# Conditioning rows summed over partitions by VectorE block turns and one small matmul, with the bias as a first row of the sum

## The chip, the core and the metric

The kernel runs on one core of a Trainium2 chip. The metric is the device time of one execution in microseconds (us). The engines spoken of are TensorE (PE in the profile, with PEld for its weight loads), VectorE (DVE), ScalarE (ACT), GpSimd (POOL) and SyncE (SP), whose queue issues nearly all DMA transfers. Every engine works through its own instructions strictly in order.

## The reference

Two transformer stacks of two layers each run one after the other on 256 tokens of width 1024; the first one also carries 256 context tokens through its first layer. Every layer is steered by a conditioning vector: a matrix-vector product gives six rows of 1024 values, of which two shift (`sh`), two scale (`sc`) and two gate (`g`) the layer.

```python
mod = silu_c @ w_ada[l] + b_ada[l]            # 1024 x 6144, once per layer (and once for the context)
sh_a, sc_a, g_a, sh_f, sc_f, g_f = jnp.split(mod[:, None, :], 6, axis=-1)
hx = rmsnorm(x) * (1 + sc_a) + sh_a
...                                           # mixing layer, attention and so on
x = x + g_a * (mixed @ w_out[l])
x = x + g_f * swiglu(rmsnorm(x) * (1 + sc_f) + sh_f, w_gate[l], w_up[l], w_down[l])
# swiglu(h, wg, wu, wd) = (silu(h @ wg) * (h @ wu)) @ wd,  1024 -> 2816 -> 1024
```

All is fp32.

## The kernel before

**Weights.** A large matrix product is cut into weight chunks. `weights` loads a chunk (`raw`, 128x1024 for two row blocks of 512 columns; some are 768 or 512 wide), ScalarE rounds it to `whi` (L170) and VectorE takes the rest, `wlo = raw - whi` (L171, both in `split`). TensorE multiplies each piece three times: high by high, high by low, low by high (L177, L178, L179 in `mm3`). In the first feed-forward each of `raw`, `whi` and `wlo` has three buffers, so a chunk can be made ready while TensorE works on one of the two before. In the later feed-forwards spoken of here there are six for the high and low parts. A chunk of two row blocks in the first feed-forward (four groups of 128 tokens) is 24 matmuls of 512 columns.

**Modulations beside the matmuls.** Some of the conditioning rows are worked out in small steps beside the three feed-forwards that come before their use. `ada_one` is a Python generator for one job, one row of 1024 values: for each of eight blocks `k` it loads 128x1024 of the matrix (`adaw`, three buffers) and VectorE accumulates `acc += adaw * cs` (L358, the first block with L356), `cs` holding 128 values of the conditioning vector, one for each partition. A job for two vectors (the main and the context tokens) has two `acc`, both fed from one `adaw`. Then the bias is added in partition 0 (L364) and the sum over the 128 partitions is taken:

- for a gate (`g`): two halves, each split into `acchi` and `acclo` and multiplied on TensorE by a matrix of ones (L372, L373);
- for a shift or scale (`sh`, `sc`), which is needed as a column of 128 partitions by 8: eight TensorE transposes of 128x128 in two groups of four (L382), each group followed by four ScalarE copies that sum along the row (L387, `colj`, into `cols`); then one VectorE copy (`col_out`, L249 or L251).

**Order.** `tick` is called once for each weight chunk and adds `rate` to a counter; for each whole number in it one step of the front job is emitted, up to its next `yield`. The first feed-forward (`ffn0`, about 298 to 668 us) has 12 jobs at 1.8 steps for each of its 64 chunks, three of them with two `acc`; the second (`1`, about 860 to 1060 us) has five at 0.75, the third (`b0`, about 1160 to 1300 us) two at 0.45. That makes 19 jobs with 22 `acc`: 14 for shifts and scales, 8 for gates. `ffn` empties the list of jobs before its last product (`tick(all_=True)`, L828 and L831). From the stream that comes of it a scheduler with its own estimates of time fixes the order on every engine when the kernel is built; the orders shown below are its result.

```python
def tick(self, all_=False):
    self.due += self.rate
    while self.jobs and (all_ or self.due >= 1.0):
        self.due -= 1.0
        if next(self.jobs[0], "end") == "end":
            self.jobs.pop(0)
```

Of the kernel before, what the change touches and what calls it, by code (L numbers as in the profile page):

```python
# [12 lines left out]
F32 = mybir.dt.float32  # L13
F32R = mybir.dt.float32r
U32 = mybir.dt.uint32
AF = mybir.ActivationFunctionType
ALU = mybir.AluOpType
AX = mybir.AxisListType
PSUM = bass.MemoryType.PSUM

P = 128
D = 1024
KT = D // P
# [71 lines left out]
class Net:  # L95
# [90 lines left out]
    def setup(self, fp):  # L186
        nc, A, cp = self.nc, self.A, self.cp
        self.ident = self.t(cp, [P, P], F32, "ident")
        make_identity(nc, self.ident)
        self.ones = self.t(cp, [P, P], F32R, "ones")  # L190
        nc.vector.tensor_scalar(self.ones, self.ident, 0.0, 1.0, op0=ALU.mult, op1=ALU.add)
        self.mhalf = self.t(cp, [P, 16], F32, "mhalf")
        nc.vector.memset(self.mhalf, -0.5)

        self.cs = self.t(cp, [P, 24], F32, "cs")
        self.bcol = self.t(cp, [P, 6, KT], F32, "bcol")
        with self.tc.tile_pool(name="rows", bufs=1) as rp:
            rows = self.t(rp, [64, P], F32, "rows")
            cols = lambda a: a.rearrange("(k p) -> k p", p=P)
            for i, s in ((0, A["c"][0]), (1, A["c_ctx"]), (2, A["b_ada"][0])):  # L200
                n = s.shape[0] // P
                nc.scalar.dma_start(out=rows[8 * i : 8 * i + n], in_=cols(s))
            ps = self.tr_bank()
            nc.tensor.transpose(ps[:, :64], rows, self.ident[:64, :64])
            nc.scalar.activation(self.cs[:, :16], ps[:, :16], AF.Silu)
            nc.vector.tensor_copy(self.bcol, ps[:, 16:64].rearrange("p (j k) -> p j k", j=6))

        self.cs32 = self.t(fp, [P, KT, 32], F32, "cs32")
        nc.vector.memset(self.cs32, 0.0)
        nc.vector.tensor_copy(  # L210
            self.cs32[:, :, :2], self.cs[:, :16].rearrange("p (c k) -> p k c", c=2)
        )

        self.pick = self.t(cp, [P, 2], F32, "pick")
        nc.vector.reduce_sum(
            self.pick, self.ident.rearrange("p (g m) -> p m g", g=4)[:, :2], axis=AX.X
        )
        self.sel = self.t(fp, [P, 2, P], F32, "sel")
        nc.vector.tensor_copy(self.sel, self.pick.unsqueeze(2).to_broadcast([P, 2, P]))
# [120 lines left out]
    def ada_one(self, pool, w, b, j, pairs):  # L340


        nc = self.nc
        kind = ("sh", "sc", "g")[j % 3]
        dests = [self.mod_dest(m, j, pool if c == 1 else None) for m, c in pairs]
        accs = [self.t(pool, [P, D], F32, "acc", bufs=2) for _ in pairs]
        brow = self.t(pool, [1, D], F32, "brow", bufs=1)
        nc.sync.dma_start(out=brow, in_=b[j * D : j * D + D].unsqueeze(0))
        for k in range(KT):
            raw = self.t(pool, [P, D], F32, "adaw", bufs=3)  # L350
            nc.sync.dma_start(out=raw, in_=w[k * P : k * P + P, j * D : j * D + D])
            for acc, (_, c) in zip(accs, pairs):
                s = self.cs[:, c * 8 + k : c * 8 + k + 1]
                with self.tc.issue_after(self.anchor):
                    if k == 0:
                        nc.vector.tensor_scalar_mul(acc, raw, s)  # L356
                    else:
                        nc.vector.scalar_tensor_tensor(  # L358
                            acc, raw, s, acc, op0=ALU.mult, op1=ALU.add
                        )  # L360
                if k > 0:
                    yield
        for acc, dest in zip(accs, dests):
            nc.vector.tensor_add(acc[0:1], acc[0:1], brow)  # L364
            if kind == "g":
                for h in range(2):
                    s = slice(h * 512, h * 512 + 512)
                    hi = self.t(pool, [P, 512], F32R, "acchi", bufs=1)
                    lo = self.t(pool, [P, 512], F32R, "acclo", bufs=1)
                    self.split(hi, lo, acc[:, s])  # L370
                    ps = self.ac_bank()
                    nc.tensor.matmul(ps, self.ones, hi, start=True, stop=False)  # L372
                    nc.tensor.matmul(ps, self.ones, lo, start=False, stop=True)  # L373
                    nc.scalar.copy(dest[:, s], ps)
            else:
                junk = self.t(pool, [P, P], F32, "colj", bufs=1)
                cols = self.t(pool, [P, KT], F32, "cols", bufs=2)
                for h in range(2):
                    ps = self.ac_bank()
                    for i in range(4):  # L380
                        k = 4 * h + i
                        nc.tensor.transpose(  # L382
                            ps[:, i * P : i * P + P], acc[:, k * P : k * P + P], self.ident
                        )
                    for i in range(4):
                        k = 4 * h + i
                        nc.scalar.activation(  # L387
                            junk, ps[:, i * P : i * P + P], AF.Copy, accum_out=cols[:, k : k + 1]
                        )
                self.col_out(kind, cols, dest)  # L390

    def side_jobs(self, jobs=(), rate=0.0):

# [1487 lines left out]
```

## Time and profile before

| what | value |
|---|---|
| median of 3 runs | 1702.78 us (1700.35 to 1704.63) |
| the profiled execution | 1704.78 us |
| its span, first to last instruction | 1703.0 us |
| mean granted TensorE clock | 0.990 of full speed |
| busy: PE, DVE, ACT, POOL | 96%, 72%, 50%, 3% of the span |

The span leaves out 1.8 us of the profiled execution's time. That execution lies 2.0 us above the median of the runs. Busy shares are means over stages with different limits; a stage has to be read by itself.

### The profile page before, as it was taken

The page shows a single profiled execution, that of the slowest core. Times are in us where ns is not written, and L with a number is a line of the kernel's source. Part 1 is how long each engine was busy: PE and PEld are TensorE (multiplying, and loading weights), DVE is VectorE, ACT ScalarE, POOL GpSimd, SP SyncE. Part 2 cuts the span into 40 slices and gives each one's busy share as a digit, 9 for nine tenths or more (in the row PEclk, how much of TensorE's full clock was granted, in tenths as well). Part 3 has the DMA queues.
Part 4 walks back from the last instruction along what each step waited for, and adds up shares of the span by engine and source line. Part 5 has one row for each costly group of instructions (what it writes and reads, how often), then busy time and mean ns, then how long its engine had stood idle before and what let it go on. Part 6 is the DMA issues. An engine that isn't in the chain of part 4 may idle for free.

```text
span 1703.0 us, 25231 instructions
## 1 busy us (share of the span) xinstructions
PE 1637.8 (96%) x9299; PEld 1313.0 (77%) x9299; DVE 1221.2 (72%) x2042; ACT 854.0 (50%) x1697; POOL 44.7 (3%) x53
## 2 busy tenths in 40 slices
PE   8999999999999999999999999999999999899998
PEld 5777767877777877787678878777877888778886
DVE  4558866886978877878768887887766567575555
ACT  4445664533333334555764455686544456564443
POOL 0001100000000000101000000000000000000000
PEclk9999999999999999999999999999999999999999
DMA  9550415554778786522268887434875543255653
GB/s 319 188 174 26 159 60 189 179 191 143 226 234 299 253 275 208 163 79 89 71 202 287 302 311 250 152 122 124 260 247 179 188 137 92 83 177 168 203 166 115
DMA packets 169474, 310.35 MB, mean 182 GB/s; under 512 B 12163, under 2 KB 72819, under 8 KB 169350
## 3 DMA queue, kind: packets, MB, share of 16 engines
q1 hardware_dynamic: 168966, 308.17, 56.3%
q8 instruction: 73, 1.20, 0.3%
q10 hardware_dynamic: 384, 0.56, 0.1%
q14 instruction: 51, 0.42, 0.1%
HBM read 307.64 MB, written 1.05 MB: 181 GB/s over the span
## 4 chain that ended last, share of the span: by engine, by line
PE 71%; DVE 10%; DMA 9%; ACT 5%; issue 3%; POOL 1%; SPq 0%; POOLq 0%; ACTq 0%; DVEq 0%
PE bank L179 19%; PE bank L177 19%; PE bank L178 19%; DVE wlo L171 3%; ACT whi L170 2%; PE bank L936 2%; DMA raw<-w_up 2%; PE bank L863 2%; DVE acc L358 1%; DMA adaw<-w_ada 1%; DMA raw<-w_gate 1%; PE bank L1478 1%; PE bank L321 1%; PE bank L1004 1%; ACT colj L387 1%
## 5 line engine op out<-in xcount | busy, mean ns | idle before, releaser
L170 ACT CAST whi<-raw 128x1024 fp32r<-128x1024 f32 (+2 forms) x420 | 400.5, 959 | 521.7 <-PE bank L179 239.7
L171 DVE TENSOR_TENSOR wlo<-raw,whi 128x1024 fp32r<-128x1024 f32 (+2 forms) x420 | 463.6, 1109 | 247.0 <-ACT whi L170 239.6
L177 PE MATMUL bank<-whi,hh 128*128 128x512 f32 (+2 forms) x1200 | 445.1, 374 | 10.7 <-ACT hh L170 5.8
L178 PE MATMUL bank<-wlo,hh 128*128 128x512 f32 (+2 forms) x1200 | 443.5, 370 | 2.1 <-DVE wlo L171 2.1
L179 PE MATMUL bank<-whi,hl 128*128 128x512 f32 (+2 forms) x1200 | 442.2, 371 | 0.2 <-DVE hl L171 0.2
L177 PEld LDWEIGHTS bank<-whi,hh 128*128 128x128 f32 x1200 | 228.0, 191 | 50.1 <-ACT hh L170 7.8
L179 PEld LDWEIGHTS bank<-whi,hl 128*128 128x128 f32 x1200 | 229.0, 191 | 36.1 <-DVE hl L171 3.5
L178 PEld LDWEIGHTS bank<-wlo,hh 128*128 128x128 f32 x1200 | 229.0, 191 | 33.8 <-DVE wlo L171 3.2
L358 DVE SCALAR_TENSOR_TENSOR acc<-adaw,cs,acc 128x1024 f32<-128x1024 f32 x154 | 196.0, 1279 | 18.1 <-DMA adaw<-w_ada 8.8
L178 PE MATMUL bank<-wlo,acth 128*128 128x512 f32 x440 | 174.5, 397 | 0.5 <-DVE wlo L171 0.5
L177 PE MATMUL bank<-whi,acth 128*128 128x512 f32 x440 | 174.9, 398 | 0.0
L179 PE MATMUL bank<-whi,actl 128*128 128x512 f32 x440 | 173.6, 395 | 0.0
L177 PE MATMUL bank<-hh,whi 128*128 128x512 f32 (+1 forms) x376 | 143.3, 382 | 0.0
L178 PE MATMUL bank<-hl,whi 128*128 128x512 f32 (+1 forms) x376 | 143.0, 381 | 0.0
L179 PE MATMUL bank<-hh,wlo 128*128 128x512 f32 (+1 forms) x376 | 142.5, 382 | 0.2 <-DVE wlo L171 0.2
L179 PEld LDWEIGHTS bank<-whi,actl 128*128 128x128 f32 x440 | 83.2, 189 | 18.6
L177 PEld LDWEIGHTS bank<-whi,acth 128*128 128x128 f32 x440 | 83.2, 189 | 18.5
L178 PEld LDWEIGHTS bank<-wlo,acth 128*128 128x128 f32 x440 | 83.2, 189 | 18.5 <-DVE wlo L171 0.9
L179 PEld LDWEIGHTS bank<-hh,wlo 128*128 128x128 f32 x376 | 70.1, 188 | 15.1 <-DVE wlo L171 0.4
L178 PEld LDWEIGHTS bank<-hl,whi 128*128 128x128 f32 x376 | 70.6, 188 | 14.4
L177 PEld LDWEIGHTS bank<-hh,whi 128*128 128x128 f32 x376 | 70.5, 188 | 14.5
L736 DVE TENSOR_TENSOR rtmp<-bank,gate 128x512 f32<-128x512 f32 x68 | 46.5, 686 | 32.4 <-PE bank L179 32.4
(297 smaller groups left out, 1867.6 us busy)
## 6 DMA issues: line engine op xcount, KB each, us to landing
adaw<-ada_w SPq DMA_DIRECT2D x96, 512.0 KB
adaw<-w_ada SPq DMA_DIRECT2D x80, 512.0 KB
raw<-ffn_w_in SPq DMA_DIRECT2D x64, 512.0 KB
raw<-w_down SPq DMA_DIRECT2D x46, 512.0 KB
raw<-ffn_w_out SPq DMA_DIRECT2D x40, 512.0 KB
raw<-w_gate SPq DMA_DIRECT2D x32, 512.0 KB
raw<-w_up SPq DMA_DIRECT2D x32, 512.0 KB
raw<-w_in SPq DMA_DIRECT2D x56, 256.0 KB
```

The source lines that it names most:

```text
L170: a = self.nc.scalar.copy(hi, src)
L171: b = self.nc.vector.tensor_sub(lo, src, hi.bitcast(F32))
L177: mm(out, lh, rh, start=start, stop=False)
L178: mm(out, lh, rl, start=False, stop=False)
L179: mm(out, ll, rh, start=False, stop=stop)
L321: nc.tensor.matmul(ps[h][32 * g : 32 * g + 32], self.cs32[:, k0 + g], raws[g][:, h * 512 : h * 512 + 512], start=k0 == 0, stop=k0 > 0,)
L358: nc.vector.scalar_tensor_tensor(acc, raw, s, acc, op0=ALU.mult, op1=ALU.add)
L387: nc.scalar.activation(junk, ps[:, i * P : i * P + P], AF.Copy, accum_out=cols[:, k : k + 1])
L736: nc.vector.tensor_mul(tmp[:, :nw], ps[:, :nw], gate[:, n0 : n0 + nw])
L863: self.nc.tensor.transpose(ps[:, i * P : i * P + P], ps_in[:, i * P : i * P + P], self.ident)
L936: self.nc.tensor.matmul(o[e * 64 : e * 64 + 64], v, pt[:, e::2, i], start=i == 0, stop=i == len(vs) - 1)
L1004: nc.tensor.transpose(ps[:, h * P : h * P + P], qn[:, h0 + h].bitcast(F32), self.ident)
```

## The change

The sum over partitions for a shift or scale is taken in another way. VectorE turns `acc` in blocks of 32 by 32 (`nc.vector.transpose`, STREAM_TRANSPOSE, 128x1024) and sums along each block's row (TENSOR_REDUCE to 128x32): that leaves four partial sums for each value, one in each group of 32 partitions. Then the job yields, and at its next step one matmul of 128x128 by 32 columns with the constant `fold` adds the four, and four small copies of 32 partitions by 8 spread the result out. Gates keep their matmuls with ones, with a `yield` after each split.

The bias is no longer added at the end: `brow` is now 128x1024, set to zero by GpSimd with the bias loaded into its row 0, and the first accumulation takes it as its addend (so L356 and L364 go, and every block is a SCALAR_TENSOR_TENSOR). The yields change too: one for each block `k`, for all `acc` of the job at once, where before there was one for each `acc` and block except the first. With the yields at the end, a job with one `acc` has 10 steps (shift, scale) or 11 (gate) in place of 8, and one with two has 11 or 13 in place of 15. The rates are as before.

```diff
+        self.fold = self.t(cp, [P, 4, 32], F32, "fold")
+        nc.vector.reduce_sum(
+            self.fold[:, 0], self.ident.rearrange("p (a i) -> p i a", a=4), axis=AX.X
+        )
+        nc.vector.tensor_copy(
+            self.fold[:, 1:], self.fold[:, :1].to_broadcast([P, 3, 32])
+        )
...
-        brow = self.t(pool, [1, D], F32, "brow", bufs=1)
-        nc.sync.dma_start(out=brow, in_=b[j * D : j * D + D].unsqueeze(0))
+        brow = self.t(pool, [P, D], F32, "brow", bufs=1)
+        nc.gpsimd.memset(brow, 0.0)
+        nc.sync.dma_start(out=brow[0:1], in_=b[j * D : j * D + D].unsqueeze(0))
...
                 with self.tc.issue_after(self.anchor):
-                    if k == 0:
-                        nc.vector.tensor_scalar_mul(acc, raw, s)
-                    else:
-                        nc.vector.scalar_tensor_tensor(
-                            acc, raw, s, acc, op0=ALU.mult, op1=ALU.add
-                        )
-                if k > 0:
-                    yield
+                    nc.vector.scalar_tensor_tensor(
+                        acc, raw, s, acc if k else brow, op0=ALU.mult, op1=ALU.add
+                    )
+            yield
         for acc, dest in zip(accs, dests):
-            nc.vector.tensor_add(acc[0:1], acc[0:1], brow)
             if kind == "g":
...
                     self.split(hi, lo, acc[:, s])
+                    yield
                     ps = self.ac_bank()
...
-                junk = self.t(pool, [P, P], F32, "colj", bufs=1)
-                cols = self.t(pool, [P, KT], F32, "cols", bufs=2)
-                for h in range(2):
-                    ps = self.ac_bank()
-                    for i in range(4):
-                        k = 4 * h + i
-                        nc.tensor.transpose(
-                            ps[:, i * P : i * P + P], acc[:, k * P : k * P + P], self.ident
-                        )
-                    for i in range(4):
-                        k = 4 * h + i
-                        nc.scalar.activation(
-                            junk, ps[:, i * P : i * P + P], AF.Copy, accum_out=cols[:, k : k + 1]
-                        )
-                self.col_out(kind, cols, dest)
+                turned = self.t(pool, [P, D], F32, "colj", bufs=1)
+                part = self.t(pool, [P, 32], F32, "cols", bufs=2)
+                nc.vector.transpose(turned, acc)
+                nc.vector.reduce_sum(
+                    part, turned.rearrange("p (b j) -> p b j", j=32), axis=AX.X
+                )
+                yield
+                ps = self.ac_bank()
+                nc.tensor.matmul(
+                    ps[:, :32], self.fold.rearrange("p a i -> p (a i)"), part, start=True, stop=True
+                )
+                for a in range(4):
+                    r = slice(32 * a, 32 * a + 32)
+                    self.col_out(
+                        kind, ps[r, :32].rearrange("p (k a) -> p a k", a=4)[:, a], dest[r]
+                    )
```

Line numbers of the changed kernel are 8 to 10 higher than those of before: L358 becomes L365, L443 L452, L457 L466, L474 L483, L736 and L737 become L745 and L746; the turn is L386, its reduction L387, the fold matmul L392. Numbers at the end of a name count the program's buffers and differ a little between the two.

**Place A, VectorE at the start of the first feed-forward.** Before, between the low parts of its second and third weight chunk (`wlo_3563`, `wlo_3597`; `xn` and `ynorm` are the normalised rows of the residual, `hl` their low parts, `rstd` a reciprocal root):

```order
L171 TENSOR_TENSOR wlo_3563<-raw_3560,whi_3562 128x1024
L443 TENSOR_SCALAR rstd_3431<-ss_3428 128x1
L358 SCALAR_TENSOR_TENSOR acc_3526<-adaw_3533,cs_82,acc_3526 128x1024
L457 TENSOR_SCALAR xn_3427<-resx_3027,rstd_3431 128x512 x2
L358 SCALAR_TENSOR_TENSOR acc_3525<-adaw_3567,cs_82,acc_3525 128x1024
L474 TENSOR_SCALAR ynorm_3441<-bank_688_3436,cols_0x_106 128x256
L474 TENSOR_SCALAR ynorm_3451<-bank_690_3446,cols_0x_106 128x256
L171 TENSOR_TENSOR wlo_3597<-raw_3594,whi_3596 128x1024
```

Now, ending with the same chunk's low part under its new name `wlo_3602`:

```order
L452 TENSOR_SCALAR rstd_3434<-ss_3431 128x1
L365 SCALAR_TENSOR_TENSOR acc_3529<-adaw_3567,cs_85,acc_3529 128x1024
L466 TENSOR_SCALAR xn_3430<-resx_3030,rstd_3434 128x512 x2
L365 SCALAR_TENSOR_TENSOR acc_3528<-adaw_3571,cs_85,acc_3528 128x1024
L483 TENSOR_SCALAR ynorm_3444<-bank_689_3439,cols_0x_109 128x256
L483 TENSOR_SCALAR ynorm_3454<-bank_691_3449,cols_0x_109 128x256
L365 SCALAR_TENSOR_TENSOR acc_3529<-adaw_3571,cs_85,acc_3529 128x1024
L171 TENSOR_TENSOR hl_2405<-ynorm_3444,hh_2404 128x2x256
L171 TENSOR_TENSOR hl_2405<-ynorm_3454,hh_2404 128x2x256
L483 TENSOR_SCALAR ynorm_3464<-bank_693_3459,cols_0x_109 128x256
L483 TENSOR_SCALAR ynorm_3474<-bank_695_3469,cols_0x_109 128x256
L171 TENSOR_TENSOR wlo_3602<-raw_3599,whi_3601 128x1024
```

One accumulation, two low parts of normalised rows and two normalisations have moved ahead of the third chunk's low part.

**Place B, VectorE at the end of the first feed-forward.** Before, the last job's last accumulation and the low parts of the last product's chunks stand so:

```order
L358 SCALAR_TENSOR_TENSOR acc_6144<-adaw_6243,cs_82,acc_6144 128x1024
L364 TENSOR_TENSOR acc_6144<-acc_6144,brow_6145 1x1024
L171 TENSOR_TENSOR wlo_6273<-raw_6270,whi_6272 128x1024
L171 TENSOR_TENSOR wlo_6291<-raw_6288,whi_6290 128x1024
```

Now they are mixed up with the last job (`rtmp` and `resc` add a product to the residual):

```order
L365 SCALAR_TENSOR_TENSOR acc_6120<-adaw_6136,cs_85,acc_6120 128x1024
L171 TENSOR_TENSOR wlo_6211<-raw_6208,whi_6210 128x512
L365 SCALAR_TENSOR_TENSOR acc_6120<-adaw_6139,cs_85,acc_6120 128x1024
L745 TENSOR_TENSOR rtmp_6217<-bank_1190_6158,gate_3527 128x512
L365 SCALAR_TENSOR_TENSOR acc_6120<-adaw_6142,cs_85,acc_6120 128x1024
L746 TENSOR_TENSOR resc_3034<-resc_3034,rtmp_6217 128x512
L365 SCALAR_TENSOR_TENSOR acc_6120<-adaw_6145,cs_85,acc_6120 128x1024
L745 TENSOR_TENSOR rtmp_6229<-bank_1191_6159,gate_3527 128x512
L386 STREAM_TRANSPOSE colj_6148<-acc_6120 128x1024
L746 TENSOR_TENSOR resc_3034<-resc_3034,rtmp_6229 128x512
L387 TENSOR_REDUCE cols_6149<-colj_6148 128x32
L171 TENSOR_TENSOR wlo_6237<-raw_6234,whi_6236 128x1024
```

The last job's turn and reduction now stand directly ahead of `wlo_6237`, a chunk in the middle of the last product. Ahead of this piece, from the low part of the last chunk of the up matrix (`wlo_6071`, 128x768) on, there stand seven more accumulations (the last four of them the last job's first ones), one more turn with its reduction, the low parts `wlo_6163`, `wlo_6181` and `wlo_6199` of 128x1024, six operations of 512 columns (`sg`, `actl`) and four small copies.

TensorE at the same place now has the fold matmul right before the first use of that chunk's low part:

```order
L179 MATMUL bank_1191_6159<-whi_6210,actl_5511 128x512
L177 MATMUL bank_1206_6232<-whi_6236,acth_5510 128x512
L177 MATMUL bank_1207_6233<-whi_6236,acth_5510 128x512
L392 MATMUL bank_1189_6152<-cols_6149,fold_78 128x32
L178 MATMUL bank_1206_6232<-wlo_6237,acth_5510 128x512
L179 MATMUL bank_1206_6232<-whi_6236,actl_5511 128x512
```

It has moved in there together with the job; before, transposes stood at this end of the stage.

## Rows read from the trace of the kernel before

**Rows 1.** The page: busy us, share of the span and instructions of each engine.
```profile
PE 1637.8 (96%) x9299; PEld 1313.0 (77%) x9299; DVE 1221.2 (72%) x2042; ACT 854.0 (50%) x1697; POOL 44.7 (3%) x53
```
**Rows 2.** Windows: stretch, length, busy time (instructions) by engine, granted clock, DMA share, GB/s.
```profile
298.00:668.00 370.00, 366.29 (x1681) 295.23 (x1680) 299.75 (x335) 144.02 (x317) 2.33 (x2) 1.00 0.69 225
860.00:1060.00 200.00, 195.55 (x926) 162.34 (x925) 161.13 (x183) 102.58 (x177) 1.11 (x2) 1.00 0.81 274
...
318.00:425.00 107.00, 106.29 (x509) 86.71 (x510) 84.37 (x98) 45.69 (x87) 0.00 (x0) 1.00 0.53 169
```
**Rows 3.** Waits: engine and line, what for, us in total, times, longest.
```profile
PEld bank L382 <- ACT colj L387: 11.0, 16, 2.8
```
**Rows 4.** Timeline of TensorE around one pair of groups: start, length, instruction.
```profile
410.27 0.39 PE L178 MATMUL bank<-wlo,acth 128*128 128x512 f32 x1
410.50 0.40 PE L179 MATMUL bank<-whi,actl 128*128 128x512 f32 x1
...
411.41 0.40 PE L178 MATMUL bank<-wlo,acth 128*128 128x512 f32 x1
...
413.02 0.40 PE L179 MATMUL bank<-whi,actl 128*128 128x512 f32 x1
413.55 0.66 PE L382 MATMUL bank<-ident,acc 128*128 128x128 f32 x4
...
414.27 0.39 PE L178 MATMUL bank<-wlo,acth 128*128 128x512 f32 x1
```
**Rows 5.** Groups that touch `acc`: count, shortest, median and longest in ns.
```profile
L382 PE MATMUL bank<-ident,acc x112: 270/273/332, 410.7 to 1254.2; 128*128 128x128 f32 x112
...
L356 DVE TENSOR_SCALAR acc<-adaw,cs x22: 734/746/754, 305.8 to 1242.7; 128x1024 f32<-128x1024 f32 x22
L364 DVE TENSOR_TENSOR acc<-acc,brow x22: 1203/1207/1214, 346.2 to 1287.5; 1x1024 f32<-1x1024 f32 x22
```
**Rows 6.** Timeline of TensorE late in `b0`; brackets: idle before, and until what.
```profile
1251.07 0.40 PE L177 MATMUL bank<-whi,acth 128*128 128x512 f32 x1
1253.81 0.66 PE L382 MATMUL bank<-ident,acc 128*128 128x128 f32 x4 [2.34 <-ACT colj L387]
...
1254.62 0.63 PE L179 MATMUL bank<-whi,actl 128*128 128x512 f32 x1
...
1257.61 0.51 PE L177 MATMUL bank<-whi,acth 128*128 128x512 f32 x1
```
**Rows 7.** Timeline of VectorE at place A.
```profile
304.69 1.23 DVE L171 TENSOR_TENSOR wlo<-raw,whi 128x1024 fp32r<-128x1024 f32 x1 [2.02 <-ACT whi L170]
305.83 0.75 DVE L356 TENSOR_SCALAR acc<-adaw,cs 128x1024 f32<-128x1024 f32 x1
...
318.08 1.22 DVE L171 TENSOR_TENSOR wlo<-raw,whi 128x1024 fp32r<-128x1024 f32 x1
```
**Rows 8.** VectorE's groups in 298 to 668: count, busy us, mean ns, idle before.
```profile
L358 DVE SCALAR_TENSOR_TENSOR acc<-adaw,cs,acc 128x1024 f32<-128x1024 f32 x105 | 133.4, 1280 | 17.3 <-DMA adaw<-w_ada 8.8 <-DMA adaw<-ada_w 7.7
L171 DVE TENSOR_TENSOR wlo<-raw,whi 128x1024 fp32r<-128x1024 f32 x52 | 63.3, 1219 | 30.3 <-ACT whi L170 30.3
...
L812 DVE TENSOR_TENSOR sg<-bank,sg 128x512 f32<-128x512 f32 x22 | 14.7, 684 | 0.6
```
**Rows 9.** Two lines of other stages, columns as in rows 5.
```profile
L979 DVE TENSOR_REDUCE hss<-hsq x14: 274/286/686, 124.5 to 805.3; 128x2 f32<-128x128 f32 x8, 128x8 f32<-128x512 f32 x6
...
L1133 DVE COPY_PREDICATED hatt<-mask,bank x72: 287/296/306, 59.8 to 796.8; 128x128 f32<-128x128 uint32 x72
```
**Rows 10.** Timeline of TensorE at place A.
```profile
319.35 0.39 PE L179 MATMUL bank<-hh,wlo 128*128 128x256 f32 x1
```
**Rows 11.** Timeline of ScalarE at place B.
```profile
648.49 0.83 ACT L170 CAST whi<-raw 128x768 fp32r<-128x768 f32 x1 [1.62 <-DMA raw<-w_up]
```
**Rows 12.** Timeline of VectorE at place B.
```profile
649.36 0.96 DVE L171 TENSOR_TENSOR wlo<-raw,whi 128x768 fp32r<-128x768 f32 x1 [0.50 <-ACT whi L170]
...
668.20 1.23 DVE L171 TENSOR_TENSOR wlo<-raw,whi 128x1024 fp32r<-128x1024 f32 x1 [1.66 <-ACT whi L170]
```

## Prediction

> **What bounds the kernel now.** I read the page's head first: TensorE is busy for 96% of the span [rows 1]. Then the windows, stage by stage, because a mean over stages says nothing of one: in the first feed-forward TensorE works 366.29 of 370 us and VectorE 299.75, in the second TensorE 195.55 of 200 [rows 2]. So time can be won only by taking work or waits from TensorE, and VectorE's slack, 70 us of 370, must carry what is moved to it. Then the waits: TensorE's weight load for the transposes L382 waits 16 times for the ScalarE copies L387, 11.0 us [rows 3]. Then the timelines of the places where the new order differs most, A and B. A change of under 5 us (0.3%) is about what a measurement of this kernel cannot tell from none.
>
> **Removed from TensorE.** Matmuls of 512 columns start every 0.23 us at the full clock [rows 4] (0.229 over longer stretches of the same timeline). Where a group of four transposes stands without a wait, the start before it and the second start behind it lie 0.91 us apart in place of 0.46: the group costs 0.45 us. Where it waits for the copies, 1.25 in place of 0.46: 0.79 us [rows 4]. There are 112 transposes [rows 5], so 28 groups, and 16 waits [rows 3]. One of them is the long one in `b0`: from 1251.07 to 1254.62 are 3.55 us for two further matmuls (0.46), so 3.1 us are lost there; behind it eight starts (seven steps) take 2.99 us in place of 1.60, since the clock has fallen to 1.2 GHz, another 1.4 us [rows 6]. Sum: 12 × 0.45 + 15 × 0.79 + 3.1 = 20.4, and 1.4 for the clock. **Gain 21.8 us.**
>
> **Added to TensorE.** 14 fold matmuls. No row shows one; a quarter of an unhindered group is 0.11 and a whole one 0.45 us [rows 4]. I take 0.2, nearer to one instruction than to four: 2.8 us (1.5 to 6.3).
>
> **Moved on VectorE.** Durations overlap by 0.07 to 0.09: `wlo` lasts 1.23 and its successor starts 1.14 later [rows 7]. So an accumulation counts 1.21, a `wlo` of 1024 columns 1.15, an operation of 512 columns 0.61 [rows 8]. Removed are 22 multiplications of 0.67 and 22 bias additions of 1.14 [rows 5], in their place come 22 more accumulations of 1.21: 13 us less. Added are 14 turns and 14 reductions of 1024 columns, and three copies more each. The trace has a reduction of 512 columns, 0.686 at most, beside 0.684 for any 512-column operation [rows 8, 9], so one of 1024 goes with the 1.22 of `wlo`: 1.15 as it counts. The turn no row shows. Below it is a pass over 1024 columns with one tensor input, 0.746 [rows 5]; above, eight operations of 128x128 at 0.296 [rows 9], 2.4 us. I take 1.2, the commonest price of 1024 columns, 1.15 in a stream. Turns, reductions and copies then are 14 × 2.7 = 38 us, net 25 us more on VectorE, some 17 of it in `ffn0` (10 of the 14 sums, 15 of the 22 `acc`): 317 of 370 us. By the mean that is hidden. The order decides where it isn't.
>
> [...]
>
> **Place A.** Between the low parts of the first and the third chunk VectorE now does one accumulation (1.2), two accumulations in place of multiplications (1.07), two more `ynorm` (0.9) and two `hl` (1.22) before the third, 4.4 us more; 0.9 of that falls into its waits for `rstd`. `wlo_3597` ended at 319.3 and TensorE used it at 319.35 [rows 7, 10], so there is no cover: its successor comes 3.5 us later, and TensorE gets 0.4 back by doing transposes meanwhile. **Loss 3.1 us** (1.5 to 4.4).
>
> **Between A and B.** A double job now feeds both its `acc` in one step, so at 1.8 steps for each chunk early chunks have up to 3.6 accumulations. Over the 18 chunks behind `wlo_3602` the new order has 42 accumulations (50.8), 18 `wlo` (20.7), 27 operations of 512 columns (16.5), four turns and three reductions (8.1) and some 18 tiny ones (2.4), 98.5 us. TensorE needs 18 × 24 × 0.229 = 99 us for the same. Before, VectorE was busy for only 84.37 of 107 us there [rows 2]. So it keeps up, but with nothing in hand, and a wait for an `adaw` now reaches TensorE. Over `ffn0` those waits were 17.3 us [rows 8]. I take 1.5 us (0 to 9).
>
> **Place B.** The emptying of the job list ahead of the last product now meets 13 steps, all of the last job and the end of the one before, since the list has 128 steps for 64 × 1.8 = 115; before, 117, two over. From the low part of the last chunk of the up matrix to `wlo_6237` VectorE has 11 accumulations (13.3), four `wlo` of 1024 (4.6), one of 768 (0.9) and one of 512 (0.6), two turns and two reductions (4.6), ten operations of 512 (6.1) and four copies (0.6): 30.7 us. It cannot begin earlier: the chunk's buffers come free when TensorE begins the chunk two before, and the cast of 0.83 [rows 11] goes ahead. From there to the fold matmul and the first use of `wlo_6237` TensorE has 54 + 42 matmuls, 0.2 and two more: 22.6 us. 30.7 + 0.9 − 22.6 = **loss 9.0 us**. Before, the same piece had VectorE waiting for ScalarE, 0.50 at its start and 1.66 before 668.20 [rows 12]: it was ahead. With a turn at 0.67 the loss is 8, at 2.4 11.5.
>
> **Other edits.** The memsets run on GpSimd, busy 2.33 us of 370 [rows 2]; the cost is nothing while a job lasts several chunks, and with that cover gone a late `brow` stops the first accumulation and VectorE behind it. In the second feed-forward 52 steps meet about 42 from the rate, so a whole job is left, but six buffers let VectorE go ahead: 0 (to 4). `b0` ends with 21 of 25. Waits of a few us at A and B may bring the clock down as in [rows 6]: two falls of about 1.6, 3.2 us (0 to 5).
>
> **Sum.** −21.8 + 2.8 + 3.1 + 1.5 + 9.0 + 3.2 = −2.2 us, from the profiled 1704.8: 1702.6. The median lies 2.0 lower: 1700.6.
>
> **Rivals.**
> 1. *Given back at A and B* (forecast): 1700.6, its own range 1697.7 to 1708. Chance 0.40.
> 2. *Faster: the end of `ffn0` costs half.* If turn and reduction cost 0.67 each, or VectorE's pieces overlap more than I count, B is 5 to 7, A 1.5, the middle nothing and no clock falls: −21.8 + 2.8 + 1.5 + 6 = −11.5, median 1691; with no loss at all 1684. For it: VectorE has 70 us of slack [rows 2]. Against: the slack lies where the order does not put the work. Chance 0.37.
> 3. *Slower: the double jobs overfill VectorE.* The first 18 chunks have 98.5 of 99 us. If the 8.8 us of waits for `w_ada` [rows 8] fall there in place of my 1.5, the sum is +5, median 1708; a turn of 2.4 adds 1.2 for each of four there and 2.5 at B, 1715. It decides from about 9 us lost there. Against: before, only a little of the waiting lay in these chunks, since VectorE was busy for 84 of 107 us and mostly ahead. Chance 0.23.
> 4. *The fold is no cheaper than the transposes:* a wait for the reduction takes the place of that for the copies in each of 14 sums. With 0.79 each it is 11 us in place of 2.8, median 1709; as the matmul comes one step, half a chunk or more, behind its reduction, I count it within the third, not apart.
>
> Faster 0.37, same 0.40, slower 0.23. The range reaches to the middle of the faster case and to 1711 in the slower one: 1687 to 1711.
>
> **What would show it.** Turn and reduction at 1.2 us each in the groups; TensorE without any wait over 1 us between A and B; an idle of some 3 us before the third chunk at A (L179, released by `wlo`), and two idles of together 9 us at the end of `ffn0`, the larger before the fold matmul L392, followed by matmuls at 1.2 GHz. I am wrong if B shows less than 5 us, or if TensorE idles for many short times in the first 100 us of `ffn0`.

## The result, and the profile after

The changed kernel takes 1718.51 us (median of 4 runs, 1716.25 to 1721.68) against 1701.57 (median of 4, 1699.06 to 1704.63) for the kernel before: a ratio of 1.0095, 95% interval 1.0081 to 1.0109. It is slower by about 16 us, on the other side of the forecast and outside its range. The profiled executions are 1718.94 and 1704.78 us, 14.2 us apart.

The page's head shows no bound that has moved. Columns as in [rows 1], spans first:

```profile
span 1717.2 us, 24943 instructions
...
PE 1630.3 (95%) x9215; PEld 1310.5 (76%) x9215; DVE 1244.1 (72%) x2092; ACT 815.9 (48%) x1473; POOL 63.1 (4%) x72
```

TensorE has 7.5 us less to do than in [rows 1] and takes 14 us longer: it waits, or runs at a lower clock (mean granted clock 0.984, before 0.990). VectorE's busy share is the same 72%, so a mean could not have told this.

To see where, I took the start of each of the 9155 matmuls that both kernels share, other than those of the modulations, and subtracted the time before from the time after. This lag, in us, stands here at some places of the span (time in the kernel before), for the changed kernel and for the experiments below, from one profile of each; the last column is the last matmul:

```
time before        310    352    396    648    677    896    963   1085   1308    end
changed           -1.8   +5.9   +4.8   -5.3   +6.5   +6.0   +3.2  +15.5  +11.9  +14.2
e1_rates          -2.8   +9.1   +7.6   +2.2   +0.7   +3.8   +2.0   +5.6   +0.9   +1.3
e2_steps          -3.4   +1.9   +2.8   -1.2   +7.6   +7.3   +4.5  +14.6  +11.8  +14.1
e3_bias           -1.8   -1.0   -1.1   +2.3   +2.3   +1.8   -0.1   +1.3   +3.4   +5.5
e4_oldsteps       -2.6   -1.8   -1.9  -10.0   -9.8   -8.7  -11.2   -7.1   -9.6  -10.0
e5_late_fold      -2.6   -1.5   -1.5  -10.2  -10.9  -10.9  -11.1   -6.1  -12.7  -14.2
e6_two_turns      -0.5   +0.7   +0.6   -0.7   +6.0   +9.0   +7.1  +14.0   +9.3  +10.2
e7_dense_doubles  +0.3  +12.1  +22.4  +15.1  +13.4  +14.1  +12.6  +18.5  +16.9  +17.8
e8_burst          -2.3   -1.2   -1.2  -12.5   +5.8   +7.8   +5.0  +10.1   +9.2   +8.1
e9_old_bias       -2.6   -2.6   -2.6   -7.0   -6.1   -5.0   -4.0   +3.7   -1.8   -2.0
e10_slow_second   -0.3   +0.9   +0.8   -6.8   -6.6   -6.5   -8.5   -2.4   -7.3   -7.2
e11_fast_second   -1.9   -0.7   -0.8   -8.0   -8.6   -8.3   -4.4   +7.2   -0.6   -1.1
e12_adaw4         +1.0   +1.7   +1.7   -8.0   -9.5   -8.4  -11.2   -8.9  -15.0  -15.3
```

Read the first line from left to right: 7.7 us are lost at place A (310 to 352), 11.2 won in the middle of the first feed-forward (352 to 648), 11.8 lost at place B (648 to 677) and 9.5 in the second feed-forward (896 to 1085). A row's small steps, up to 2 or 3 us, also occur where two kernels do not differ (the column 310): they are the scatter of single executions. A profile is also one execution among several: those of e4_oldsteps and e5_late_fold took 5.2 and 2.8 us less than the median of their runs, those of e3_bias, e6_two_turns, e7_dense_doubles and e10_slow_second 4.9, 6.4, 4.4 and 3.5 more. So a row shows where time goes, and the ratios below show how much.

**The prices.** Groups in the changed kernel, with columns as in [rows 5]:

```profile
L386 DVE STREAM_TRANSPOSE colj<-acc x14: 1230/1236/1246, 382.9 to 1257.7; 128x1024 f32<-128x1024 f32 x14
```

```profile
L387 DVE TENSOR_REDUCE cols<-colj x14: 1202/1208/1220, 385.2 to 1260.0; 128x32 f32<-128x1024 f32 x14
```

Turn and reduction cost what a subtraction of 1024 fp32 columns costs (1.22, L171), 1.24 and 1.21 us; the 1.2 I took was right. The upper bound of 2.4 us, eight operations of 128x128 [rows 9], is about twice the measured price.

**Place A.** TensorE at the start of the first feed-forward; in brackets the idle before and what ended it:

```profile
312.36 0.41 PE L473 MATMUL bank<-ident,xn 128*128 128x128 f32 x2 [0.56 <-DVE xn L466]
...
314.91 0.87 PE L473 MATMUL bank<-ident,xn 128*128 128x128 f32 x6 [0.75 <-DVE xn L466]
...
317.55 1.74 PE L473 MATMUL bank<-ident,xn 128*128 128x128 f32 x8 [1.77 <-ACT ynorm L485]
...
320.95 0.33 PE L244 MATMUL bank<-ident,rows 40*128 40x40 f32 x1 [1.66 <-ACT ynorm L485]
...
321.87 0.58 PE L179 MATMUL bank<-hh,wlo 128*128 128x256 f32 x1 [0.20 <-DVE wlo L171]
```

The idles are 4.94 us. Before they were 1.87, at the same places:

```profile
312.04 0.41 PE L464 MATMUL bank<-ident,xn 128*128 128x128 f32 x2 [0.68 <-DVE xn L457]
313.48 0.38 PE L179 MATMUL bank<-hh,wlo 128*128 128x256 f32 x1 [0.20 <-DVE wlo L171]
315.73 0.87 PE L464 MATMUL bank<-ident,xn 128*128 128x128 f32 x6 [0.26 <-DVE xn L457]
318.37 0.33 PE L464 MATMUL bank<-ident,xn 128*128 128x128 f32 x1 [0.73 <-ACT ynorm L476]
```

The difference is 3.1 us. The idle before the L179 that waits for `wlo` is 0.20 in both kernels; what has grown stands before transposes that wait for ScalarE's `ynorm` (L485). ScalarE in turn had waited for VectorE's `ynorm` (L483; 1.36 us before the second of the two), which in the order of place A stands behind accumulations and low parts; VectorE's trace has these lines in that order, from `rstd` at 312.52 to `wlo` at 320.61.

The clock does the rest, as windows of the changed kernel show (columns as in [rows 2]); in 318 to 330 before, the granted clock was 1.00, now it was 0.50 from 318 to 328:

```profile
318.00:330.00 12.00, 10.02 (x55) 9.38 (x54) 10.37 (x18) 6.47 (x11) 0.00 (x0) 0.58 0.50 142
655.00:680.00 25.00, 15.96 (x55) 12.19 (x54) 22.69 (x32) 6.89 (x11) 0.00 (x0) 0.80 0.51 166
1005.00:1022.00 17.00, 12.10 (x44) 8.99 (x43) 14.22 (x15) 6.46 (x8) 0.95 (x1) 0.80 0.77 248
```

**Place B.** TensorE at the end of the first feed-forward:

```profile
657.38 0.62 PE L177 MATMUL bank<-whi,acth 128*128 128x512 f32 x2
661.16 0.51 PE L178 MATMUL bank<-wlo,acth 128*128 128x512 f32 x1 [3.17 <-DVE wlo L171]
...
669.30 0.62 PE L177 MATMUL bank<-whi,acth 128*128 128x512 f32 x2
675.36 0.60 PE L392 MATMUL bank<-cols,fold 128*128 128x32 f32 x2 [5.44 <-DVE cols L387]
676.40 0.80 PE L178 MATMUL bank<-wlo,acth 128*128 128x512 f32 x1 [0.44 <-DVE wlo L171]
```

Three idles, 9.05 us, the longest before the fold matmul; VectorE works through most of the longest without a break, in the order of place B:

```profile
670.48 1.28 DVE L365 SCALAR_TENSOR_TENSOR acc<-adaw,cs,acc 128x1024 f32<-128x1024 f32 x1
671.68 0.68 DVE L745 TENSOR_TENSOR rtmp<-bank,gate 128x512 f32<-128x512 f32 x1
672.28 1.23 DVE L386 STREAM_TRANSPOSE colj<-acc 128x1024 f32<-128x1024 f32 x1
673.44 0.65 DVE L746 TENSOR_TENSOR resc<-resc,rtmp 128x512 f32<-128x512 f32 x1
674.01 1.21 DVE L387 TENSOR_REDUCE cols<-colj 128x32 f32<-128x1024 f32 x1
675.13 1.21 DVE L171 TENSOR_TENSOR wlo<-raw,whi 128x1024 fp32r<-128x1024 f32 x1
```

The reduction ends at 675.2, the fold starts at 675.36.

**The second feed-forward.** TensorE's waits there, after:

```profile
PE bank L827 <- DVE sg L821: 8.3, 5, 3.0
```

and before, for the same lines under their old numbers:

```profile
PE bank L818 <- DVE sg L812: 1.7, 3, 0.6
```

L827 are the transposes of `sg`, the product of gate and up matrix. VectorE ahead of the two longest of these waits:

```profile
1004.07 1.22 DVE L171 TENSOR_TENSOR wlo<-raw,whi 128x1024 fp32r<-128x1024 f32 x1
1005.20 1.24 DVE L386 STREAM_TRANSPOSE colj<-acc 128x1024 f32<-128x1024 f32 x1
1006.37 1.18 DVE L171 TENSOR_TENSOR wlo<-raw,whi 128x1024 fp32r<-128x1024 f32 x1
1007.47 1.21 DVE L387 TENSOR_REDUCE cols<-colj 128x32 f32<-128x1024 f32 x1
1008.60 0.68 DVE L821 TENSOR_TENSOR sg<-bank,sg 128x512 f32<-128x512 f32 x1
...
1012.74 1.22 DVE L171 TENSOR_TENSOR wlo<-raw,whi 128x1024 fp32r<-128x1024 f32 x1 [2.33 <-ACT whi L170]
1013.88 1.28 DVE L365 SCALAR_TENSOR_TENSOR acc<-adaw,cs,brow 128x1024 f32<-128x1024 f32 x1
1015.08 0.68 DVE L171 TENSOR_TENSOR actl<-bank,acth 128x512 fp32r<-128x512 f32 x1
1015.68 0.68 DVE L821 TENSOR_TENSOR sg<-bank,sg 128x512 f32<-128x512 f32 x1
```

The first product stands behind turn and reduction. The second stands behind a `wlo` that itself waits 2.33 us: its cast waited for the load of its weights, 5.09 us, as ScalarE's timeline shows:

```profile
1011.66 1.04 ACT L170 CAST whi<-raw 128x1024 fp32r<-128x1024 f32 x1 [5.09 <-DMA raw<-w_gate]
```

Two more of the waits come at the end of the stage:

```profile
1058.35 0.55 PE L827 MATMUL bank<-ident,sg 128*128 128x128 f32 x3 [1.39 <-DVE sg L821]
...
1061.15 0.55 PE L827 MATMUL bank<-ident,sg 128*128 128x128 f32 x3 [1.32 <-DVE sg L821]
```

The stage's last job, the one left over by the rate, begins on VectorE at 1051.81. Its accumulations at 1055.42 and 1058.22, each with one `wlo` behind it, stand directly ahead of the two products (1057.75 and 1060.54). So the stage loses time at two places: 3.7 us are won between 896 and 992, then the lag grows by 7.4 between 992 and 1019 and by some 6 between 1040 and 1085.

### The profile page after: what moved, and what is told of

Read it like the earlier page. It is cut to its first block, busy times and chain, and to the rows that moved or that the text cites. A ratio compares the mean times of both kernels' runs of the same rounds, so it can differ in the third digit from the quotient of the medians.

```text
span 1717.2 us, 24943 instructions
## 1 busy us (share of the span) xinstructions
PE 1630.3 (95%) x9215; PEld 1310.5 (76%) x9215; DVE 1244.1 (72%) x2092; ACT 815.9 (48%) x1473; POOL 63.1 (4%) x72
## 5 line engine op out<-in xcount | busy, mean ns | idle before, releaser
L171 DVE TENSOR_TENSOR wlo<-raw,whi 128x1024 fp32r<-128x1024 f32 (+2 forms) x420 | 462.8, 1108 | 253.8 <-ACT whi L170 252.7
L179 PE MATMUL bank<-whi,hl 128*128 128x512 f32 (+2 forms) x1200 | 442.5, 371 | 0.0
L179 PEld LDWEIGHTS bank<-whi,hl 128*128 128x128 f32 x1200 | 228.5, 190 | 35.9 <-DVE hl L171 3.2
L365 DVE SCALAR_TENSOR_TENSOR acc<-adaw,cs,acc 128x1024 f32<-128x1024 f32 x154 | 195.5, 1278 | 9.6 <-DMA adaw<-w_ada 5.4
L179 PE MATMUL bank<-whi,actl 128*128 128x512 f32 x440 | 174.7, 397 | 0.0
L179 PE MATMUL bank<-hh,wlo 128*128 128x512 f32 (+1 forms) x376 | 144.4, 386 | 0.2 <-DVE wlo L171 0.2
L179 PEld LDWEIGHTS bank<-whi,actl 128*128 128x128 f32 x440 | 84.0, 191 | 18.6
L179 PEld LDWEIGHTS bank<-hh,wlo 128*128 128x128 f32 x376 | 71.9, 192 | 15.1 <-DVE wlo L171 0.3
L745 DVE TENSOR_TENSOR rtmp<-bank,gate 128x512 f32<-128x512 f32 x68 | 46.7, 687 | 32.0 <-PE bank L179 31.3
```

What stands on the lines that cost most here:

```text
L171: b = self.nc.vector.tensor_sub(lo, src, hi.bitcast(F32))
L179: mm(out, ll, rh, start=False, stop=stop)
L365: nc.vector.scalar_tensor_tensor(acc, raw, s, acc if k else brow, op0=ALU.mult, op1=ALU.add)
L745: nc.vector.tensor_mul(tmp[:, :nw], ps[:, :nw], gate[:, n0 : n0 + nw])
```

## The experiments

Theory 1 was that the time is lost where the new number of steps puts the jobs: a denser start (A), and steps left over when the lists are emptied (B and the second feed-forward). Theory 2: VectorE's added work costs time wherever it stands. Theory 3: the bias row. Ratios are to the kernel before, run in between on the same chip.

**Two higher rates** (e1_rates), on the changed kernel:

```diff
-            self.side_jobs(jobs, 1.8)
+            self.side_jobs(jobs, 2.02)
...
-            (A["w_gate"][1], A["w_up"][1], A["w_down"][1]), ada2[5:10], .75, hp, (b0, 0),
+            (A["w_gate"][1], A["w_up"][1], A["w_down"][1]), ada2[5:10], .97, hp, (b0, 0),
```

> The changed kernel with the two rates raised (1.8 to 2.02, 0.75 to 0.97), so that the job lists are empty before the last products. Theory 1 (the time was lost where the job lists are emptied at once: 11.7 us of lag at the end of the first feed-forward, at least 5 in the second): the idles before the fold matmul and before the last product vanish, about 1718 - 12 - 5 = 1701 us, 1697 to 1706. Theory 2 (the 38 us of turns and reductions on VectorE cost the same wherever they stand): 1714 to 1720. Theory 3 (the bias row, its memset and its wait): no change either, 1714 to 1720. Against theory 1 also: if the denser early chunks overfill VectorE, 1706 to 1714 with many idles in the first 100 us of that stage.

Measured: 1.0017 (1.0000 to 1.0034). Place B is gone: from 648 to 677 the lag falls by 1.5 us, and TensorE has no wait between 640 and 687. The second feed-forward loses 1.8 in place of 9.5, and nothing between 1040 and 1085. Place A is dearer, 11.9 in place of 7.7. So of the two rates theory 1 had the ends right, and its own reserve, the denser start, came true too.

**The new steps with the old sums** (e2_steps), on the kernel before:

```diff
-                if k > 0:
-                    yield
+            yield
...
                     self.split(hi, lo, acc[:, s])
+                    yield
...
             else:
+                yield
                 junk = self.t(pool, [P, P], F32, "colj", bufs=1)
```

> The kernel before, with its transposes and its bias addition, but with the changed kernel's yields alone (one for each block, one ahead of each sum over partitions), so that the job lists have the changed kernel's number of steps. Theory 1: slower than before by most of the loss without any of the gain from the transposes; the emptying at the end of the first feed-forward meets 13 steps, VectorE's stretch there is shorter by two turns and reductions (4.6 us), so 4 to 8 us lost there and 3 to 10 in the second: 1708 to 1720 us. Theories 2 and 3: nothing but order changes, 1698 to 1704.

Measured: 1.0077 (1.0051 to 1.0103). With the transposes, the bias addition and all of VectorE's operations as before, the yields alone lose 5.3 us at A, 8.8 at B and 7.3 in the second feed-forward. That is most of the result, and none of it is the turn's doing.

**The bias row alone** (e3_bias), on the kernel before:

```diff
-        brow = self.t(pool, [1, D], F32, "brow", bufs=1)
-        nc.sync.dma_start(out=brow, in_=b[j * D : j * D + D].unsqueeze(0))
+        brow = self.t(pool, [P, D], F32, "brow", bufs=1)
+        nc.gpsimd.memset(brow, 0.0)
+        nc.sync.dma_start(out=brow[0:1], in_=b[j * D : j * D + D].unsqueeze(0))
...
-                    if k == 0:
-                        nc.vector.tensor_scalar_mul(acc, raw, s)
-                    else:
-                        nc.vector.scalar_tensor_tensor(
-                            acc, raw, s, acc, op0=ALU.mult, op1=ALU.add
-                        )
+                    nc.vector.scalar_tensor_tensor(
+                        acc, raw, s, acc if k else brow, op0=ALU.mult, op1=ALU.add
+                    )
...
-            nc.vector.tensor_add(acc[0:1], acc[0:1], brow)
```

> The kernel before with the bias row alone: memset on GpSimd, bias in row 0, first accumulation with that row as its addend; yields and transposes as before. VectorE has 22 x (0.67 + 1.14 - 1.21) = 13 us less to do. Theories 1 and 2: within 3 us of before, 1698 to 1703. Theory 3: 1707 to 1718.

Measured: 1.0014 (0.9994 to 1.0035): no difference that shows. Theory 3 falls.

**The new sums with the old steps** (e4_oldsteps), on the changed kernel:

```diff
-            yield
+                if k > 0:
+                    yield
...
                     self.split(hi, lo, acc[:, s])
-                    yield
...
-                yield
                 ps = self.ac_bank()
```

> The changed kernel with the yields of before (one for each accumulation but those of the first block, none at the end), so that rates and steps fit as before; turn, reduction and fold matmul are emitted in one step. Theory 1: no bursts, the transposes' 21.8 us are gained and each of 14 folds may wait for its reduction where the order leaves too little between them (0 to 1 us each): 1683 to 1697. Theory 2: 1710 to 1718. Theory 3: 1710 to 1718.

Measured: 0.9972 (0.9950 to 0.9993). The same operations as in the changed kernel, 1.2% faster than it by their places alone. A costs 0.8 us, B nothing. But the gain is short of the 5 to 19 us expected: 4.8. TensorE waits four times for the reduction, and the second feed-forward loses 1.6.

**A fold one step later, with the old number of steps** (e5_late_fold), on that kernel:

```diff
-                if k > 0:
+                if k > 0 and (kind == "g" or k > 1 or acc is not accs[0]):
                     yield
...
+                if acc is accs[0]:
+                    yield
                 ps = self.ac_bank()
```

> The run with the steps of before, but with the fold matmul emitted one step after the reduction; the yield for it is taken from the second block, so the number of steps stays 8 and 15. Theory 1 (steps that fit, and a fold that does not wait): the four waits of TensorE for the reduction in that run (3.0 us) and the clock's fall behind the longest go, ratio to before about 0.995, against 0.9972 there. Theory 2 (VectorE's added work costs what was not regained): ratio unchanged, 0.996 to 0.999.

Measured: 0.9940 (0.9925 to 0.9954), 10 us faster than before. Of the four waits one is left:

```profile
PE bank L393 <- DVE cols L387: 0.5, 1, 0.5
```

That is the changed kernel's idea, a fold behind the reduction, without its extra steps.

**Each turn done twice** (e6_two_turns), on e4_oldsteps:

```diff
                 nc.vector.transpose(turned, acc)
+                nc.vector.transpose(turned, acc)
```

> The run with the steps of before with each turn done twice (14 more of 1.24 us, 17 us on VectorE; the result is the same). Theory 1 (VectorE's added work is hidden where no burst stands): within 3 us of that run, ratio to before 0.996 to 0.999. Theory 2 (the added work costs time wherever it stands): the 17 us show by half or more, ratio 1.001 to 1.007.

Measured: 1.0019 (1.0005 to 1.0033), 0.0047 above the kernel it was made from, some 8 us for 17 us of work. Theory 1 as I had put it falls here: the added work is not hidden although the steps fit. But the run does not show that work on VectorE costs time wherever it stands. With the old steps a fold is emitted in the same step as its turn, so the second turn lies on the way to the fold: TensorE's waits for the reduction, four in either kernel, grow from 3.0 to 9.7 us. By the lag, 1.3 us are won between 396 and 648 in place of 8.1, 6.7 are lost at B in place of 0.2 (a wait of 4.35 us before a fold) and 5.0 in the second feed-forward in place of 1.6. These lags overstate it: the two profiles end 20 us apart, the medians some 8.

**The dense start alone** (e7_dense_doubles), on e4_oldsteps:

```diff
-                if k > 0:
+                if k > 0 and acc is accs[-1]:
                     yield
```

> The run with the steps of before, but with one yield for both sums of a double job, which makes the first chunks of the first feed-forward as dense as in the changed kernel and leaves no steps over at its end (96 for 115). Theory 1: the 5 to 8 us that the changed kernel lost between 310 and 352 us are back, and nothing is lost at the end of the stage: ratio to before 1.000 to 1.003. Rival (place A is the work of the bias row or of the scheduler's order): no change against 0.9972.

Measured: 1.0085 (1.0066 to 1.0103). A comes back and is far dearer than expected: 11.8 us up to 352, 22.1 up to 396, then the usual gain, and nothing at B. Here both turns and reductions of a double job also fall into one step; TensorE waits for `wlo`:

```profile
PE bank L179 <- DVE wlo L171: 12.7, 4, 6.3
```

**The burst alone** (e8_burst), on e4_oldsteps:

```diff
-            self.side_jobs(jobs, 1.8)
+            self.side_jobs(jobs, 1.62)
```

> The run with the steps of before, but with the rate of the first feed-forward lowered from 1.8 to 1.62, so that 13 steps are left at its end as in the changed kernel, with no dense start. Theory 1: 9 to 12 us are lost between 640 and 680 us and nowhere else, ratio 1.002 to 1.005. Rival (the loss needs the new yields, not the number left over): under 4 us, ratio below 1.000.

Measured: 1.0065 (1.0050 to 1.0079), above the expected band. Between 648 and 677 us 18.3 are lost, and place A shows nothing (1.1 us). So a mere number of leftover steps, with the old yields, does it. It is dearer than in the changed kernel since two folds stand directly behind their reductions:

```profile
PE bank L391 <- DVE cols L387: 10.1, 2, 5.0
```

**The old bias under the best version** (e9_old_bias), on e5_late_fold, the diff of e3_bias backwards:

```diff
-        nc.gpsimd.memset(brow, 0.0)
...
-                        acc, raw, s, acc if k else brow, op0=ALU.mult, op1=ALU.add
...
+                    if k == 0:
+                        nc.vector.tensor_scalar_mul(acc, raw, s)
...
+            nc.vector.tensor_add(acc[0:1], acc[0:1], brow)
```

> The best version so far (turn, reduction and late fold with the steps of before, ratio 0.994) with the bias taken in as before: a 128x1024 multiplication for the first block, the bias added in partition 0 at the end, no memset, no bias row. VectorE gets 13 us more to do, two thirds of it in the first feed-forward. Theory 1 (the gain is the transposes'; the bias row gives nothing): ratio 0.992 to 0.996. Rival (the 13 us less work for VectorE are part of the gain, as the doubled turns cost 8 of 17 us): ratio 0.997 to 1.001.

Measured: 0.9998 (0.9985 to 1.0012). The rival holds: without the bias row the whole gain is gone. The 13 us less work for VectorE were worth nothing beside the transposes (e3_bias) and are worth 10 us beside the turns (the order changes a little with them, so not all need be the work itself). Windows of 298 to 640 (columns as in [rows 2]) show VectorE without the bias row:

```profile
298.00:640.00 342.00, 335.56 (x1524) 272.57 (x1524) 305.31 (x358) 106.57 (x144) 2.32 (x2) 1.00 0.71 231
```

and in the best version with it:

```profile
298.00:640.00 342.00, 337.96 (x1539) 275.34 (x1538) 300.93 (x346) 108.19 (x145) 13.37 (x13) 1.00 0.71 235
```

That VectorE, 88 to 89% busy there, has no room for bunches is my reading and not shown: of the 12.2 us between the ends of the two rows only 3.2 have come up by 648, and 3.9 come in the second feed-forward.

**The rate of the second feed-forward, and a fourth buffer**, all on e5_late_fold, one line each: 0.67 in place of 0.75 (e10_slow_second), 1.0 (e11_fast_second), and

```diff
-            raw = self.t(pool, [P, D], F32, "adaw", bufs=3)
+            raw = self.t(pool, [P, D], F32, "adaw", bufs=4)
```

> The best version (late fold, steps of before, bias row) with the rate of the second feed-forward at 0.67 in place of 0.75, so some 4 of its 40 steps are left over at its end. Theory A (in the middle of that stage loads and VectorE work of the jobs meet too densely; the best version still lost some 5 us there): the middle gets better by 2 to 5 us and the end loses 0 to 3, ratio 0.992 to 0.995. Theory B (three adaw buffers: loads of weights stand in the queue behind an adaw that waits for its buffer): no change by the rate, 0.993 to 0.996.

> The best version with the rate of the second feed-forward at 1.0 in place of 0.75; its jobs end early and nothing is left over. Theory A: denser, so 3 to 8 us more lost in the middle of that stage, ratio 0.996 to 0.999. Theory B: the same, since weights wait behind more loads. If only steps left over at an end count: no change, 0.993 to 0.995.

> The best version with four adaw buffers in place of three. Theory B: the weights' loads no longer wait behind an adaw load for the accumulation three before, 2 to 5 us less in the second feed-forward, ratio 0.991 to 0.993. Theory A: no change, 0.993 to 0.995.

Measured: 0.9939 (0.9921 to 0.9957) for 0.67, 1.0014 (0.9998 to 1.0031) for 1.0, and 0.9911 (0.9896 to 0.9925) for four buffers. The lower rate changes nothing that shows in the time; by the lag it moves the loss: the 4.5 us that the best version loses between 963 and 1019 are 0.1, and 4.9 are lost between 1019 and 1040 instead. The higher one loses 12 us, more than expected, 15.5 of lag between 896 and 1085, though no step is left over. So in this stage the density of the jobs costs too, not only an emptied list. The fourth buffer gives 0.3%, 5 us. VectorE's idle time before accumulations that waited for an `adaw`, in the best version with three buffers:

```profile
DVE acc L365 <- DMA adaw<-w_ada: 6.4, 8, 1.6
DVE acc L365 <- DMA adaw<-ada_w: 6.4, 9, 1.2
```

With four, 0.8 us are left in all. By the lag the gain is where theory B had put it: in the second feed-forward the lag falls by 0.5 us in place of growing by 4.8, and ScalarE's waits there for the loads of the weights (`w_gate`, `w_up` and `w_down`, 860 to 1080 us) fall from 69.8 to 61.3 us. One wait of 2.65 us for `wlo` remains in the middle of the stage, and the lag still grows by 4.1 between 963 and 992 us. e12_adaw4 is the fastest version, 15 us ahead of the kernel before.

## Why the prediction was wrong

**Gain of the transposes: right.** In the first feed-forward I had 20 groups at 0.64 us on average less 10 folds at 0.2, 10.8 us. Of these 18 groups and 8 folds come before 648, 9.9 us, and the lag falls by 11.2 between 352 and 648.

**Prices on VectorE: right**, as shown above.

**Place A: right in the size of its waits, wrong in where they stand, short in what follows.** 3.1 us forecast, 3.1 measured as idles. VectorE's order is the cause as forecast, but I had one idle of some 3 us before L179, waiting for `wlo`; that one stayed at 0.20, and the waits came earlier, by way of `ynorm` and ScalarE. That both give 3.1 is luck. The loss is 7.7, for the clock stood at 0.58 of full in 318 to 330.

**Between A and B: right.** 1.5 forecast (0 to 9), and from 352 to 640 us no idle above 0.5. The 98.5 us against 99 held.

**Place B: right.** 9.0 forecast, 9.05 measured, with the idles where they were said to be. The agreement to a tenth is luck: VectorE's stretch, 30.7 us in the forecast, took 33.7 with 2.6 of waits in it, and TensorE's work beside it, 22.6 in the forecast, took 25.6.

**The clock: mis-sized.** I took two falls of 1.6, 3.2 us. Loss less idles gives 4.6 at A and 2.75 at B (nearer 3.6, as two groups less two folds, 0.9, are won at B too). In the second feed-forward, of the 7.4 us of lag added between 992 and 1019, 4.9 are the idles of 1.92 and 2.98, and 2.5 the clock, 0.80 in the window. About 10 us in these three, 7 more than forecast. The traces give the clock as a share of full speed and no frequency: where the prediction has 1.2 GHz, they show 0.50, behind the wait in `b0` before (1254.6 to 1257.6 us) and behind the fold at B after (675 to 679).

**The second feed-forward: the step that failed.** "A whole job is left, but six buffers let VectorE go ahead: 0 (to 4)." I counted there only `wlo`, for which the buffers are. TensorE also needs `sg` from VectorE, which can be made no earlier than its two matrix products end and has no buffer ahead; what stood in front of it in VectorE's queue became waits on TensorE, of 1.92 and 2.98 us in the middle of the stage. Nor did the buffers let VectorE go ahead where a load was late (the 2.33 us before 1012.74). With the transposes' gain there (6 groups at 0.64 less three folds, 3.2) the forecast for the stage was −3.2; it was +9.5, 12.7 us off. The waits for `sg` went from 1.7 to 8.3. Some 6 us of lag are added at the end of the stage, where the job stands that I had counted as left over and priced at nothing: in e1_rates, where no step is left over, the lag does not grow there.

**The third feed-forward: nearly, by another way.** I had 4.9 us won, and the lag falls by 3.6 between 1085 and 1308. The wait for the copies in [rows 6] went, but a wait of 2.94 us for `sg`, L827, came near it, with another fall of the clock (0.83 in 1262 to 1272).

The forecast of the profiled time was −2.2, measured are +14.2. Of the 16.4 between them 6.7 are the clock and 10.2 the rest of the second stage (12.7 less its 2.5 of clock); what is left is in the third stage, in the 1.5 that the middle did not cost, and in steps of 2 us at both ends of the span, which are scatter. The third rival had the right sign with the wrong place: the double jobs did not overfill VectorE behind A.

What the runs settle: the yields cause the loss (e2_steps has it without the turns, e4_oldsteps has the turns without it); A is the dense start (e7_dense_doubles), B the leftover (e8_burst, e1_rates). Open is the middle of the second feed-forward: kernels that differ in steps and turns lose 4 to 8 us at some place of it, e3_bias none. On the best version a higher rate makes it worse, a lower one moves it behind 1019 us, and a fourth buffer leaves 4.1 us there, though the stage as a whole then loses nothing. On the changed kernel a higher rate (e1_rates) made the stage better, since it left no step over. The fourth buffer speaks for a part of the weights' loads in it; which of VectorE's queue and these loads starts it (the DMA share in 860 to 1060 is 0.80 in e5_late_fold as in e12_adaw4) the runs do not tell apart.

## What to carry to other kernels

Count the steps when work is cut into steps that a rate deals out: a change that makes each operation cheaper can lose more by the steps left over and by steps that have become heavier than it wins. Look in the queue of the engine that has to carry moved work for products that the busy engine needs at once and that no buffer can make early. Work taken from such an engine can be worth nothing in one kernel and most of its length in another: the same 13 us were worth nothing that shows beside the transposes and 10 beside the turns.

## What was not expected of the hardware

At place A short waits cost more by the clock than by themselves: the idles grew by 3.1 us, none of them above 1.8, and from the third of them on the granted clock was 0.58 over 12 us (318 to 330; 0.50 up to 328), to which I put down the 4.6 more that were lost. Before, idles of 0.73 us and less at the same place left it at 1.00, and in e5_late_fold, where no wait listed for 298 to 700 us is longer than 1.2, it was 1.00 over 298 to 668. At place B the waits themselves cost more, 9.05 us. A turn of 128x1024 in fp32 blocks, 1.236 us, costs hardly more than a subtraction of that size, 1.22, where [rows 9] had left up to 2.4 open.
